# Modulated norm: factor on the scalar engine, scale and shift per feature behind the transposes

## The chip, the cores and the metric

The kernel runs on one core of a Trainium2 chip. The metric is the device time of one execution in microseconds (us); of several runs the median is given, and a profile belongs to one further execution. PE is TensorE (matrix multiplication), PEld its weight loads, DVE VectorE, ACT ScalarE, POOL GpSimd, SP SyncE. ACT, SP and POOL issue DMAs; in the profile q1 is the DMA queue of SP's issues, q10 that of ACT's, q0 that of POOL's. An engine name with a q (ACTq) is that engine's sequencer, which issues DMAs.

## The reference

Two blocks follow one another on 256 tokens of 1024 features, in fp32. The first has two layers of ffn, mixer, ffn, each with a residual and a layer norm. The second has two layers of a hybrid mixer and a feed-forward part (dense in layer 0, eight experts in layer 1); ahead of each stands a norm that is modulated by shift and scale rows, which are computed from a condition vector `c`:

```python
def rms_norm(x, g):
    x32 = x.astype(jnp.float32)
    y = x32 * lax.rsqrt(jnp.mean(jnp.square(x32), axis=-1, keepdims=True) + EPS)
    return (y * g.astype(jnp.float32)).astype(x.dtype)

def modulate(h, shift, scale):
    return h * (1.0 + scale) + shift

def second_block(x, c, ...):
    for layer in range(DEPTH):
        ...
        h = modulate(rms_norm(x, norm_mix_g[layer]), sh_m, sc_m)
        mix = hybrid_mixer(h, ...)
        x = x + gt_m * mix
        h = modulate(rms_norm(x, norm_ffn_g[layer]), sh_f, sc_f)
        ...
        x = x + gt_f * f
    return rms_norm(x, final_g)
```

The kernel folds `g * (1 + scale)` into one row beforehand, so that a modulated norm is x times r (one number per token) times a row, plus a row, where r is the inverse root of the mean square.

## The kernel before

The 256 tokens are two tiles, t = 0 and 1, of 128 rows by 1024 columns. To keep fp32 precision, every operand of a matmul is split in a high and a low part, and `mm3` (L175) makes three matmuls of them (L178, L179, L180). Weights come in on SP's queue in pieces of 1 MB; `weights` (L141) splits each with a Copy on ACT (L159) and a subtraction on DVE (L161). Activations are split by `split_to` (L182): a Copy on ACT (L184), a subtraction on DVE (L185).

Where a stage needs features on the partitions, `transpose_tile` (L203) turns one tile: twice four transposes on PE into one PSUM tile (L209), and each PSUM tile leaves in two parts of 128x256, each split by L184 and L185. `onward` (L1458) says what follows a stage's output: the new x is kept, the norm is applied, and `flip` transposes tile 0 at once, while tile 1's transposes are deferred to `X.complete()`, which the consumer (`toks` L279 or `ffn` L539) calls after its first matmuls on tile 0.

`ffn` (L496) makes hidden features in groups of 256 columns (f0 from 512 in the loop). Each group calls `feat_joint` (L245 and L246, into PSUM tiles of the name mm) for both weight halves, and the second weight multiplies an earlier group (`second`, into PSUM tiles of the name acc). At f0 = FF - 768 = 2048 it calls `finish.load()` (L558), which issues the loads that the residual needs; two groups and the tail follow. In the tail (L560, L562) tile 0's output is finished first, then tile 1's. `project` (L712) does the same for the mixers, with its call of load at L719.

`finish` is made by `residual_ln` (L568) or `gated_residual` (L903). The first loads ln_g and ln_b as broadcasts (`bcast` L289, an ACT-issued DMA of 512 KB at L291, kept in program order), adds the residual (L583), and applies the layer norm (L584 to L591). The second loads one gate row in the same way (`modrow` L486) and applies it (L916, L917). Both hand the tile to `then`.

`mod_norm` (L872) is used at three places, each with two tiles: behind the last ffn of the first block (residual_ln; the first mixer2 consumes it through `toks`), behind the first mixer2 (gated_residual; the dense ffn consumes it), and behind the dense ffn (gated_residual; the second mixer2 consumes it). At its first tile it issues two broadcasts of 512 KB, the shift and the scale row. Per tile, `rms` (L891) squares on ACT with a running sum (L897), DVE and POOL make r (L900, L298, L300), and then each half of 512 columns takes two passes on DVE:

```python
nc.vector.scalar_tensor_tensor(h[:, c], x[:, c], r, sc[:, c], op0=OP.mult, op1=OP.mult)   # L885
nc.vector.tensor_add(h[:, c], h[:, c], sh[:, c])                                          # L886
```

Two other places of this kernel hold patterns that the change also uses: `plan_columns` (L1109) transposes a 16x128 tile of mod rows into columns (L1113, L1115), its load being L1107 on POOL's queue; and the experts' gather applies a scale and a bias column with one Identity on ACT as data leaves PSUM (L1264), while L1168 is a Copy of a 128x1024 row tile with r as its scale.

Each engine runs its instructions in order. That order is set when the program is built: a scheduler hands out tile buffers from pools (PSUM: four of the name mm, four of the name acc; s4: 17 tiles of 4 KB per partition) and orders the instructions by what they depend on.

Of the kernel before, what the change touches and what calls it, by code (L numbers as in the profile page):

```python
# [17 lines left out]
F32 = mybir.dt.float32  # L18
# [4 lines left out]
AF = mybir.ActivationFunctionType  # L23
OP = mybir.AluOpType
# [53 lines left out]
class Kernel:  # L78
# [121 lines left out]
        x = X.parts[k // 2]  # L200
        return self.split_to(x[:, :, 0], x[:, :, 1], src)

    def transpose_tile(self, X, t, x):  # L203

        nc = self.nc
        for q in range(len(X.parts) // 2):
            p = self.mm([128, 4, 128])
            for j in range(4):
                nc.tensor.transpose(p[:, j, :], x[:, (4 * q + j) * 128:(4 * q + j + 1) * 128], self.ident)  # L209
            for i in range(2):  # L210
                part = X.parts[2 * q + i][:, :, :, t * 128:(t + 1) * 128]
                self.split_to(part[:, :, 0], part[:, :, 1], p[:, 2 * i:2 * i + 2, :])

    def transposed(self, x, nk=8):
        X = self.features(nk)
# [352 lines left out]
    def residual_ln(self, x, scale, i, then):  # L568


        nc = self.nc
        gb = []

        def load():
            gb.extend((self.bcast(self.a["ln_g"], i * D, D), self.bcast(self.a["ln_b"], i * D, D)))

        def finish(t, y):
            g, b = gb
            z = self.s4([128, D])
            st = self.s1(12)  # L580
            for n in range(2):
                c = slice(n * 512, (n + 1) * 512)
                nc.vector.scalar_tensor_tensor(z[:, c], y[n], scale / ALPHA, x[t][:, c], op0=OP.mult, op1=OP.add)  # L583
                nc.vector.bn_stats(st[:, n * 6:n * 6 + 6], z[:, c])  # L584
            mv = self.s1(2)
            nc.vector.bn_aggr(mv, st.rearrange("p (n s) -> p n s", s=6))
            r = self.rstd(mv[:, 1:2], LN_EPS / ALPHA ** 2)
            for n in range(2):
                c = slice(n * 512, (n + 1) * 512)
                nc.vector.scalar_tensor_tensor(z[:, c], z[:, c], mv[:, 0:1], g[:, c], op0=OP.subtract, op1=OP.mult)  # L590
                nc.vector.scalar_tensor_tensor(z[:, c], z[:, c], r, b[:, c], op0=OP.mult, op1=OP.add)  # L591
            then(t, z)

        finish.load = load
        return finish
# [275 lines left out]

    def mod_norm(self, l, i, then):  # L872

        nc = self.nc
        rows = []

        def norm(t, x):
            if not rows:
                rows.extend((self.modrow(l, i), self.modrow(l, i + 1)))
            sh, sc = rows  # L880
            h = self.s4([128, D])
            r = self.rms(x, h)
            for n in range(2):
                c = slice(n * 512, (n + 1) * 512)
                nc.vector.scalar_tensor_tensor(h[:, c], x[:, c], r, sc[:, c], op0=OP.mult, op1=OP.mult)  # L885
                nc.vector.tensor_add(h[:, c], h[:, c], sh[:, c])  # L886
            then(t, h)

        return norm

    def rms(self, x, scratch=None):  # L891
# [11 lines left out]
    def gated_residual(self, x, l, i, then):  # L903

        nc = self.nc
        rows = []

        def load():
            rows.append(self.modrow(l, i))

        def finish(t, y):
            g = rows[0]
            z = self.s4([128, D])
            for n in range(2):
                c = slice(n * 512, (n + 1) * 512)
                nc.vector.tensor_mul(z[:, c], y[n], g[:, c])  # L916
                nc.vector.tensor_add(z[:, c], z[:, c], x[t][:, c])  # L917
            then(t, z)

        finish.load = load  # L920
        return finish
# [536 lines left out]
    def onward(self, norm=None, fine=100):  # L1458


        x, X = [None, None], Features([])

        def flip(t, h):
            if not X.parts:
                X.parts = self.features(8).parts

            if t == 0:
                self.transpose_tile(X, t, h)
                self.fine = fine
            else:  # L1470
                X.later = lambda: self.transpose_tile(X, t, h)

        step = norm(flip) if norm else flip

        def then(t, z):
            x[t] = z
            step(t, z)

        return x, X, then

    def run(self, out):
# [68 lines left out]
```

## Time and profile before

| what | value |
|---|---|
| median of 3 runs | 2384.26 us (2381.79 to 2385.14) |
| the profiled execution | 2380.0 us |
| its span in the profile | 2378.2 us |
| mean granted PE clock | 0.996 |
| busy: PE, DVE, ACT, POOL | 98%, 81%, 63%, 3% of the span |
| DMA: SP's queue, ACT's queue | 71.0%, 1.8% of 16 engines' span |

The span is the time from the first to the last instruction in the profile; the execution's own time lies 1.8 us above it. Busy shares count an engine's instructions alone. A granted clock of 1.00 is full speed, 2.4 GHz; at about 0.5 it is at its lower level, 1.2 GHz. In the rows below, a timeline row gives the start, the busy time, engine, line, operation, what it writes and reads and the count, and in brackets the idle time before it with what ended that.

### The profile page before, as it was taken

The page shows a single profiled execution, that of the slowest core. Times are in us where ns is not written, and L with a number is a line of the kernel's source. Part 1 is how long each engine was busy: PE and PEld are TensorE (multiplying, and loading weights), DVE is VectorE, ACT ScalarE, POOL GpSimd, SP SyncE. Part 2 cuts the span into 40 slices and gives each one's busy share as a digit, 9 for nine tenths or more (in the row PEclk, how much of TensorE's full clock was granted, in tenths as well). Part 3 has the DMA queues.
Part 4 walks back from the last instruction along what each step waited for, and adds up shares of the span by engine and source line. Part 5 has one row for each costly group of instructions (what it writes and reads, how often), then busy time and mean ns, then how long its engine had stood idle before and what let it go on. Part 6 is the DMA issues. An engine that isn't in the chain of part 4 may idle for free.

```text
span 2378.2 us, 33917 instructions
## 1 busy us (share of the span) xinstructions
PE 2328.2 (98%) x12984; PEld 1992.0 (84%) x12984; DVE 1919.4 (81%) x2677; ACT 1494.7 (63%) x2172; POOL 64.5 (3%) x102
## 2 busy tenths in 40 slices
PE   8999999999999999999899999999999999999997
PEld 7888999888888999888788888878888887888876
DVE  6977877887787786887777667889989888898897
ACT  5555755564555664565475555778877777777674
POOL 0000000000000000000100001000000000000000
PEclk9999999999999999999999999999999999999999
DMA  8885446885787545677536565379999999999995
GB/s 287 301 315 178 142 161 203 273 288 182 261 286 245 183 163 184 232 258 258 181 103 227 178 203 184 116 274 329 358 336 333 351 345 342 359 334 353 365 347 208
DMA packets 318075, 607.92 MB, mean 256 GB/s; under 512 B 12976, under 2 KB 143550, under 8 KB 317904
## 3 DMA queue, kind: packets, MB, share of 16 engines
q1 hardware_dynamic: 310736, 590.52, 71.0%
q10 hardware_dynamic: 5696, 14.34, 1.8%
q8 instruction: 104, 1.70, 0.3%
q0 software_dynamic: 1472, 0.81, 0.1%
q14 instruction: 67, 0.55, 0.1%
HBM read 604.48 MB, written 1.15 MB: 255 GB/s over the span
## 4 chain that ended last, share of the span: by engine, by line
PE 39%; DVE 7%; ACT 3%; issue 2%; DMA 1%; POOL 0%; ACTq 0%; POOLq 0%; DVEq 0%
PE mm L179 7%; PE mm L180 7%; PE mm L178 7%; PE acc L179 4%; PE acc L180 4%; PE acc L178 4%; DVE wlo L161 3%; PE mm L245 3%; ACT whi L159 2%; PE mm L246 1%; PE mm L1290 1%; DVE s L185 0%; PE mm L1259 0%; DVE s L980 0%; PE mm L1339 0%
## 5 line engine op out<-in xcount | busy, mean ns | idle before, releaser
L161 DVE TENSOR_TENSOR wlo<-raw,whi 128x1024 fp32r<-128x1024 f32 (+1 forms) x1302 | 1231.6, 986 | 226.7 <-ACT whi L159 221.9
L159 ACT ACTIVATE whi<-raw 128x1024 fp32r<-128x1024 f32 (+1 forms) x1302 | 1063.4, 866 | 375.6 <-PE acc L180 95.4
L245 PE MATMUL mm<-s,whi 128*128 128x512 f32 x1440 | 510.1, 397 | 0.6 <-DVE cols L370 0.6
L179 PE MATMUL mm<-wlo,s 128*128 128x512 f32 (+1 forms) x1184 | 420.5, 356 | 3.0 <-DVE wlo L161 2.2
L178 PE MATMUL mm<-whi,s 128*128 128x512 f32 (+1 forms) x1184 | 418.8, 354 | 3.3 <-ACT s L184 2.9
L180 PE MATMUL mm<-whi,s 128*128 128x512 f32 (+1 forms) x1184 | 414.2, 351 | 1.4 <-DVE s L185 1.0
L246 PE MATMUL mm<-s,wlo 128*128 128x256 f32 x1440 | 404.1, 281 | 0.0
L179 PE MATMUL acc<-wlo,s 128*128 128x512 f32 x984 | 386.6, 395 | 1.5
L180 PE MATMUL acc<-whi,s 128*128 128x512 f32 x984 | 381.0, 392 | 0.6 <-DVE s L185 0.6
L178 PE MATMUL acc<-whi,s 128*128 128x512 f32 x984 | 377.0, 394 | 4.5 <-ACT s L184 4.5
L245 PEld LDWEIGHTS mm<-s,whi 128*128 128x128 f32 x1440 | 270.4, 188 | 67.8 <-issue 3.2
L246 PEld LDWEIGHTS mm<-s,wlo 128*128 128x128 f32 x1440 | 272.0, 189 | 2.3
L179 PEld LDWEIGHTS mm<-wlo,s 128*128 128x128 f32 x1184 | 225.3, 190 | 41.0 <-DVE wlo L161 13.8
L178 PEld LDWEIGHTS mm<-whi,s 128*128 128x128 f32 x1184 | 225.5, 190 | 35.6 <-ACT s L184 5.0
L180 PEld LDWEIGHTS mm<-whi,s 128*128 128x128 f32 x1184 | 225.0, 190 | 30.3 <-DVE s L185 1.8
L178 PE MATMUL mm<-s,whi 128*128 128x256 f32 x784 | 222.8, 285 | 1.5 <-ACT s L184 1.5
L178 PEld LDWEIGHTS acc<-whi,s 128*128 128x128 f32 x984 | 184.8, 188 | 47.0 <-ACT s L184 9.1
L179 PEld LDWEIGHTS acc<-wlo,s 128*128 128x128 f32 x984 | 185.1, 188 | 46.0 <-DVE wlo L161 9.8
L179 PE MATMUL mm<-s,whi 128*128 128x256 f32 x784 | 222.0, 283 | 0.0
L180 PE MATMUL mm<-s,wlo 128*128 128x256 f32 x784 | 221.9, 283 | 0.0
L180 PEld LDWEIGHTS acc<-whi,s 128*128 128x128 f32 x984 | 185.4, 188 | 40.8 <-DVE s L185 2.6
L178 PEld LDWEIGHTS mm<-s,whi 128*128 128x128 f32 x784 | 148.6, 190 | 3.2 <-ACT s L184 2.0
(317 smaller groups left out, 1990.6 us busy)
## 6 DMA issues: line engine op xcount, KB each, us to landing
raw<-in_moe_w_dram SPq DMA_DIRECT2D x261, 1024.0 KB, 6.2
raw<-in_ffn_w_dram SPq DMA_DIRECT2D x164, 1024.0 KB, 5.5
raw<-in_w_in_dram SPq DMA_DIRECT2D x60, 1024.0 KB, 5.0
raw<-in_ada_w_dram SPq DMA_DIRECT2D x48, 1024.0 KB, 5.3
raw<-in_w_out_dram SPq DMA_DIRECT2D x16, 1024.0 KB
s<-rows ACTq DMA_DIRECT2D x10, 512.0 KB, 7.6
raw<-in_w_branch_b_dram SPq DMA_DIRECT2D x4, 1024.0 KB
raw<-in_w_branch_a_dram SPq DMA_DIRECT2D x4, 1024.0 KB
```

The costliest lines, as they stand in the source:

```text
L159: nc.scalar.activation(h[:, c], x[:, c], AF.Copy)
L161: nc.vector.tensor_sub(l[:, c], x[:, c], h.bitcast(F32)[:, c])
L178: nc.tensor.matmul(out, lh, rh, start=start, stop=False, skip_group_check=skip)
L179: nc.tensor.matmul(out, lh, rl, start=False, stop=False, skip_group_check=skip)
L180: nc.tensor.matmul(out, ll, rh, start=False, stop=stop, skip_group_check=skip)
L245: nc.tensor.matmul(p, h, X.joint(k), start=k == 0, stop=False, skip_group_check=True)
L246: nc.tensor.matmul(p[:, 0, :], l, X(k)[0], start=False, stop=k == 7, skip_group_check=True)
L1290: nc.tensor.transpose(p[:, j, :], hid[:, j * 128:(j + 1) * 128], self.ident)
```

## The change

`mod_norm` no longer loads broadcast rows. It takes a tile `cols` of 128x16, and gets a `load` of its own, which the residual's `load` calls behind its own broadcasts: one DMA of 16 rows of 128 (shift and scale, 8 KB) on ACT's queue, a transpose on PE, a copy to `cols` on DVE. Per tile, ACT multiplies x by r (two Copies of 128x512) in place of the four DVE passes. `transpose_tile` gets `cols`, and where they are given, each 128x128 block leaves PSUM through an Identity on ACT with its scale and bias column into an SBUF tile y of the name s2; `split_to` then reads y in place of PSUM. The other users of `transpose_tile` are unchanged.

```diff
@@ -200,7 +200,7 @@
         x = X.parts[k // 2]
         return self.split_to(x[:, :, 0], x[:, :, 1], src)
 
-    def transpose_tile(self, X, t, x):
+    def transpose_tile(self, X, t, x, cols=None):
 
         nc = self.nc
         for q in range(len(X.parts) // 2):
@@ -209,7 +209,14 @@
                 nc.tensor.transpose(p[:, j, :], x[:, (4 * q + j) * 128:(4 * q + j + 1) * 128], self.ident)
             for i in range(2):
                 part = X.parts[2 * q + i][:, :, :, t * 128:(t + 1) * 128]
-                self.split_to(part[:, :, 0], part[:, :, 1], p[:, 2 * i:2 * i + 2, :])
+                y = p[:, 2 * i:2 * i + 2, :]
+                if cols is not None:
+                    y = self.s2([128, 2, 128])
+                    for j in range(2):
+                        k = 4 * q + 2 * i + j
+                        nc.scalar.activation(y[:, j, :], p[:, 2 * i + j, :], AF.Identity, scale=cols[:, 8 + k:9 + k],
+                                             bias=cols[:, k:k + 1])
+                self.split_to(part[:, :, 0], part[:, :, 1], y)
 
     def transposed(self, x, nk=8):
         X = self.features(nk)
@@ -573,6 +580,8 @@
 
         def load():
             gb.extend((self.bcast(self.a["ln_g"], i * D, D), self.bcast(self.a["ln_b"], i * D, D)))
+            if hasattr(then, "load"):
+                then.load()
 
         def finish(t, y):
             g, b = gb
@@ -871,21 +880,26 @@
 
     def mod_norm(self, l, i, then):
 
-        nc = self.nc
-        rows = []
+
+        nc = self.nc
+        cols = self.p1.tile([128, 16], F32, name="mod", bufs=2)
+
+        def load():
+            r = self.s1(128)[:16, :]
+            self.tc.keep_in_program_order(nc.scalar.dma_start(r, self.rows[l, 8 * i:8 * i + 16]))
+            p = self.mm([128, 16])
+            nc.tensor.transpose(p, r, self.ident[:16, :16])
+            nc.vector.tensor_copy(cols, p)
 
         def norm(t, x):
-            if not rows:
-                rows.extend((self.modrow(l, i), self.modrow(l, i + 1)))
-            sh, sc = rows
             h = self.s4([128, D])
             r = self.rms(x, h)
             for n in range(2):
                 c = slice(n * 512, (n + 1) * 512)
-                nc.vector.scalar_tensor_tensor(h[:, c], x[:, c], r, sc[:, c], op0=OP.mult, op1=OP.mult)
-                nc.vector.tensor_add(h[:, c], h[:, c], sh[:, c])
-            then(t, h)
-
+                nc.scalar.activation(h[:, c], x[:, c], AF.Copy, scale=r)
+            then(t, h, cols)
+
+        norm.load = load
         return norm
 
     def rms(self, x, scratch=None):
@@ -907,6 +921,8 @@
 
         def load():
             rows.append(self.modrow(l, i))
+            if hasattr(then, "load"):
+                then.load()
 
         def finish(t, y):
             g = rows[0]
@@ -1460,15 +1476,15 @@
 
         x, X = [None, None], Features([])
 
-        def flip(t, h):
+        def flip(t, h, cols=None):
             if not X.parts:
                 X.parts = self.features(8).parts
 
             if t == 0:
-                self.transpose_tile(X, t, h)
+                self.transpose_tile(X, t, h, cols)
                 self.fine = fine
             else:
-                X.later = lambda: self.transpose_tile(X, t, h)
+                X.later = lambda: self.transpose_tile(X, t, h, cols)
 
         step = norm(flip) if norm else flip
 
@@ -1476,6 +1492,8 @@
             x[t] = z
             step(t, z)
 
+        if norm:
+            then.load = step.load
         return x, X, then
 
     def run(self, out):
```

## Rows read from the trace of the kernel before

**Rows 1.** Busy time and share of each engine; the chain that ended last, by engine.

```profile
PE 2328.2 (98%) x12984; PEld 1992.0 (84%) x12984; DVE 1919.4 (81%) x2677; ACT 1494.7 (63%) x2172; POOL 64.5 (3%) x102
...
PE 39%; DVE 7%; ACT 3%; issue 2%; DMA 1%; POOL 0%; ACTq 0%; POOLq 0%; DVEq 0%
```

**Rows 2.** PE's waits: total us, times, longest us.

```profile
PE mm L209 <- DVE s L886: 10.1, 5, 5.6
```

**Rows 3.** Timeline of PE, first place, ahead of the transposes of tiles 0 and 1.

```profile
1153.36 1.23 PE L209 MATMUL mm<-ident,s 128*128 128x128 f32 x8 [1.57 <-DVE s L886]
...
1168.56 1.94 PE L209 MATMUL mm<-ident,s 128*128 128x128 f32 x8 [5.64 <-DVE s L886]
```

**Rows 4.** Windows: PE, PEld, DVE, ACT, POOL busy (count), PEclk, DMA share, GB/s.

```profile
1168.50:1172.70 4.20, 4.14 (x14) 3.67 (x15) 2.12 (x5) 1.43 (x4) 0.00 (x0) 0.51 0.03 10
1172.70:1177.00 4.30, 4.30 (x20) 3.50 (x20) 2.55 (x3) 3.18 (x3) 0.00 (x0) 1.00 0.14 26
```

**Rows 5.** Timeline of DVE, first place.

```profile
1151.20 1.41 DVE L885 SCALAR_TENSOR_TENSOR s<-s,t,s 128x512 f32<-128x512 f32 x2 [0.45 <-POOL t L300]
1152.53 1.29 DVE L886 TENSOR_TENSOR s<-s,s 128x512 f32<-128x512 f32 x2
...
1157.18 0.41 DVE L185 TENSOR_TENSOR s<-mm,s 128x256 fp32r<-128x256 f32 x1
1157.52 1.27 DVE L583 SCALAR_TENSOR_TENSOR s<-acc,s 128x512 f32<-128x512 f32 x2
```

**Rows 6.** Timelines of PE and DVE, second place.

```profile
1259.35 1.41 DVE L885 SCALAR_TENSOR_TENSOR s<-s,t,s 128x512 f32<-128x512 f32 x2 [2.22 <-DMA s<-rows]
...
1261.51 0.63 PE L209 MATMUL mm<-ident,s 128*128 128x128 f32 x4 [1.78 <-DVE s L886]
```

**Rows 7.** Groups of instructions by line and form: busy us, mean ns, idle before.

```profile
L159 ACT ACTIVATE whi<-raw 128x512 fp32r<-128x512 f32 x564 | 321.8, 623 | 206.7 <-PE acc L180 70.8 <-PE mm L179 43.9 <-PE mm L245 34.8
...
L184 ACT ACTIVATE s<-mm 128x256 fp32r<-128x256 f32 x116 | 41.6, 382 | 51.0 <-PE mm L209 33.7 <-DVE s L185 11.7 <-PE mm L1290 4.6
...
L184 ACT ACTIVATE s<-mm 128x512 fp32r<-128x512 f32 x40 | 23.8, 595 | 52.9 <-PE mm L1290 52.5
...
L1264 ACT ACTIVATE s<-mm,shsc 128x256 f32<-128x256 f32 x32 | 16.3, 562 | 13.4 <-PE mm L1259 13.4
...
L1168 ACT ACTIVATE s<-s,t 128x1024 fp32r<-128x1024 f32 x2 | 2.3, 1150 | 1.5 <-POOL t L300 1.5
```

**Rows 8.** Instructions of L1113: duration ns min/median/max, start.

```profile
L1113 PE MATMUL mm<-ident,t x1: 233/233/233, 1346.7 to 1346.7; 16*128 16x16 f32 x1
```

**Rows 9.** Timelines of ACT's issues and of PE, first and third place.

```profile
1110.36 0.45 ACTq L291 DMA_DIRECT2D s<-in_ln_b_dram  x1
...
1112.40 0.39 PE L245 MATMUL mm<-s,whi 128*128 128x512 f32 x1
1112.63 0.28 PE L246 MATMUL mm<-s,wlo 128*128 128x256 f32 x1
...
1411.94 0.33 ACTq L291 DMA_DIRECT2D s<-rows  x1
...
1414.37 0.39 PE L245 MATMUL mm<-s,whi 128*128 128x512 f32 x1
```

**Rows 10.** DMA queues in 1112:1113, 1113:1118, 1117:1118, 1258.3:1259.3, 1415:1418 (packets, MB, share).

```profile
q1 hardware_dynamic: 192, 0.39, 101.0%
...
q10 hardware_dynamic: 288, 1.05, 52.0%
...
q10 hardware_dynamic: 4, 0.01, 3.1%
...
q10 hardware_dynamic: 9, 0.02, 6.1%
...
q10 hardware_dynamic: 144, 0.52, 42.7%
...
q1 hardware_dynamic: 125, 0.22, 19.4%
```

## The prediction

> **What bounds the kernel now.** The page first [rows 1]: TensorE (PE) is busy for 98% of the span, and PE leads the chain that ended last, so the time falls only if one of PE's few pauses shrinks or PE gets less to do. The waits of PE come next, to see which pauses the change can reach [rows 2]: five waits, 10.1 us together, the longest 5.6 us, lie ahead of the transposes of L209 and end with L886, the second vector pass that the change removes. Then I read the timelines at the places where the modulated norm runs: site 1 (end of the last first-block ffn), site 2 (end of the first mixer2), site 3 (end of the dense ffn). At site 1 PE waits 1.57 us before tile 0's transposes and 5.64 us before tile 1's [rows 3]. After the long wait PE runs at a granted clock of 0.51, its lower level of 1.2 GHz, for 4.2 us, then at 1.00 [rows 4]: the same eight transposes take 1.94 us instead of 1.23 [rows 3], and half of 4.2 us, about 2 us, is lost. So site 1 holds some 9 us. At site 2 the wait is 1.78 us [rows 6]; the other two of the five, at site 3, share the rest, 10.1 - 1.57 - 5.64 - 1.78 = 1.1 us. All gains must come from these 10.1 us and the 2 us of clock.
>
> Why is the 5.64 us there? VectorE (DVE) starts tile 1's layer norm, L583, at 1157.52, directly behind the last split L185 of tile 0 [rows 5], though the accumulators of tile 1 had been finished by 1151.8, when PE fell idle [rows 3]. I read this as program order: the scheduler gives tile 1 its buffers after tile 0's. Keep this order in mind, since the new load comes into it too.
>
> **What is removed and added, on DVE and ACT.** Removed per tile: two L885 and two L886, 1.41 + 1.29 = 2.7 us by the two rows and about 2.6 us from start to end (1151.20 to 1153.82) [rows 5]. In their place ScalarE (ACT) does two row Copies of 128x512 with scale r. L1168, a Copy of 128x1024 with such a scale, takes 1.150 us [rows 7]; two halves I put at 1.35 us. The path to the transposes is shorter by 1.25 us. Six tiles free DVE of 15.6 us, but DVE counts only where PE waits for it.
>
> Added per tile: eight Identity of 128x128 with a scale and a bias column. The nearest row is L1264, 128x256 with two columns, 562 ns [rows 7]; L184 takes 382 ns for 128x256 against 595 ns for 128x512 in the same group of rows, so 128 columns less are worth about 0.107 us and the estimate is 0.455 us, 0.35 us from start to start. A part of an eviction was one L184; now it is two Identity and a Copy, about 1.15 us with its hand-over instead of 0.39. The first part comes 0.75 us later, which is on the path, since PE has just transposed. The next three are hidden where PE takes longer per part than 1.15 us: at sites 1 and 3 a part feeds six matmuls of 512 columns at 0.23 us (the distance from L245 to L246 [rows 9]), 1.38 us, so they are. At site 2 the matmuls have 256 columns; half of that, 0.7 us a part, covers nothing, and tile 1 there would lose 3 x 0.45 + 0.75 = 2.1 us if nothing else filled PE.
>
> The rows don't say that ACT is the slower engine for this: a Copy of 128x512 takes it 0.623 us, and a vector pass of that size takes DVE about 0.7 us [rows 5, 7]. The Trainium skill speaks against the change here: ScalarE: Activation LUTs, Rules for kernel authors, wants add and mul on VectorE and not on ScalarE, for VectorE's rate per element in bf16. By that rule ACT would become the limit, and the sum would be that of rival 3.
>
> **Gains, site by site.** Site 1, tile 0: the Copies start when r is there (1151.20 [rows 5]) and ACT's weight split under way is done (up to 0.6 us, half of which I take), so the path is about 1 us shorter; less 0.75 us, -0.3 us. Tile 1: -1.25 us for the passes, +0.75 us for the eviction, and half of DVE's 2.6 us arrives as an earlier L583: -1.8 us. The bounds are wide: -0.5 us if the slower splits hold L583 back, -7.5 us if all 5.64 us and the clock go; I am nearer to the first, since L583 follows tile 0's splits, which get slower. Site 2: -1.78 us at tile 0 (there DVE waited for the broadcast rows, 2.22 us [rows 6], which go), half of it kept after the slower eviction, and tile 1's loss about half covered: -0.5 us, bounds -1.8 to +2.1. Site 3: -0.3 us, bounds -1.1 to +0.75. Together -2.9 us.
>
> **The new load, the decisive part.** Per site two broadcasts of 512 KB go (the pairs of L291), and one DMA of 8 KB comes, r. It is moved: the broadcasts were issued with the norm, after the last group; r is issued with the residual's own rows, two feature groups and the tail earlier, behind them on ACT's queue. A transpose of r on PE (L1113 is such a one, 0.233 us [rows 8]) and a small DVE copy follow. Both are cheap: 3 x 0.23 = 0.7 us. Their wait is not. r's PSUM tile is taken ahead of those of the next feat_joint, and if buffers go out in order of first use, no later mm tile can pass it: PE, which runs in order, stands before the transpose until r is there, with all of feat_joint behind it; DVE's copy waits with L161's weight splits behind it.
>
> When is r there? At site 1 ln_g and ln_b are issued up to 1110.36 + 0.45; r would follow at about 1110.8. feat_joint begins at 1112.40 with no pause [rows 9]. In 1112 to 1113 only q1, SP's weights, moves (101%); the ACT queue's 288 packets (1.05 MB, ln_g and ln_b) come in 1113 to 1118, the last four after 1117 [rows 10]. r's packets stand behind these. At site 2 nine packets of the broadcast rows still ran after 1258.3 [rows 10], and the waiting L885 began at 1259.35 [rows 6]: I add 1.0 us from the last packet to the release. r is usable at 1118.1; PE could have gone on at 1112.6 after the transpose: stall 5.5 us. Bounds: 0.5 us if r overtakes, 6.5 us if the transpose stands before the group's end. After 5.6 us of idleness the clock cost 2 us [rows 3, 4]; I take 1.8 us more. Site 3: one gate row ahead of r, issued at 1411.94, moved in 1415 to 1418: its 42.7% and q1's 19.4% of the engines' time [rows 10], done without a gap, end at about 1416.9; feat_joint begins at 1414.37 [rows 9]: (1416.9 + 1.0) - 1414.6 = 3.3 us, and 0.5 us for the clock (between site 2, where 1.78 us cost nothing, and site 1); bounds 0 to 5.5. Site 2: a gate row too, but there the load falls into the last projection, whose accumulations need no new mm tile and run on beside it: 0.8 us, bounds 0 to 3.
>
> Sum: 5.5 + 1.8 + 3.3 + 0.5 + 0.8 + 0.7 = +12.6 us, less 2.9 = **+9.7 us**. On the profiled execution's 2380.0 us (span 2378.2 and 1.8 around it) that is 2389.7; that execution lies 4.3 us under the median of 2384.26, so the forecast is 2394.0 us. A difference under 0.2%, 4.8 us, can't be told from none.
>
> **Rivals.**
> 1. The load is hidden: r, being 8 KB, lands early or its transpose is placed later. For it: r is 8 KB behind 512 KB pieces, and the page tells nothing of such a load on ACT's queue; against: q10's rows. Then 0.7 - 2.9 = -2.2 us: 2382, no measurable change.
> 2. Faster: r hidden, and L583 of tile 1 moves by all 2.6 us. Site 1: -0.3 - (2.6 + 1.25 - 0.75) - 2.0 of clock = -5.4; sites 2 and 3 -1.8; transposes +0.7: -6.5 us, 2377.8. It decides if r is usable by about 1112.6 and L583 starts before 1156. For it: DVE is busy without a gap at site 1; against: the order of buffers.
> 3. ACT is the path, without the stall: row Copies queue behind L159 and gain nothing, each of six first parts costs 0.75 us, site 2 loses 0.45 x 3 twice: 4.5 + 2.7 + 0.7 = +7.9 us, 2392.2.
>
> **Chances.** Forecast 0.62; rival 1 0.18; rival 2 0.12; rival 3 0.08. From them: faster 0.12, same 0.20, slower 0.68. The stall alone spans 2388 to 2400 (all upper bounds with hardly any gain); the range takes in rival 1 and leaves out rival 2: 2380 to 2400.
>
> **What would show it.** Right: in the waits of PE a new wait of the r transpose on the DMA, 5 to 6 us at site 1 and about 3 us at site 3, just before feat_joint of the last but one group, with a lower granted clock after it at site 1; PE's waits for L886 gone and replaced by shorter ones for ACT's row Copies (about 4 us left before tile 1 of site 1); Identity near 0.45 us; ACT's busy time up by some 31 us (6 x (8 x 0.455 + 1.35) and a little), DVE's down by 15.6. Wrong: r lands within 2 us of its issue, feat_joint runs ahead of the r transpose, or tile 1's L583 starts 2 us sooner.

## The result, and the profile after

The changed kernel takes 2396.38 us (median of 5 runs, 2393.72 to 2398.45) against 2384.73 us of the kernel before (5 runs on the same chip). The ratio is 1.0056, 95% interval 1.0045 to 1.0066, so 0.56% or some 13.3 us slower (10.7 to 15.7); the two medians lie 11.65 us apart. The forecast was 2394.0 us in 2380 to 2400: slower, by the load's stall. The profiled execution took 2397.67 us, its span 2395.9 us.

The page of the changed kernel, parts 1 and 3: busy time of the engines, then packets, MB and share of ACT's DMA queue.

```profile
PE 2341.2 (98%) x12987; PEld 2001.3 (84%) x12987; DVE 1905.6 (80%) x2656; ACT 1516.8 (63%) x2232; POOL 67.7 (3%) x102
...
q10 hardware_dynamic: 4928, 11.22, 1.4%
```

Against [rows 1] DVE has 13.8 us less, ACT 22.1 us more, ACT's queue moves 3 MB less. All three are what the change is said to do, and none of them says why the time grew. PE's instructions grew by three, its busy time by 13 us: part of PE's work ran at a lower clock.

The waits of PE in the changed kernel, longest in total first (us in total, times, longest us):

```profile
PE mm L891 <- DMA t<-rows: 8.0, 2, 4.7
PE mm L178 <- ACT s L184: 7.5, 6, 3.3
PE mm L209 <- ACT s L899: 5.9, 5, 2.5
```

The waits of L209 for L886 [rows 2], 10.1 us, have become 5.9 us for ACT's row Copies (L899), and a new first line stands above them: the transpose of r (L891) waits for r's DMA, in two waits of 8.0 us together. The second line was 4.5 us in three waits before. The timeline of PE at the two places:

```profile
1117.41 0.39 PE L180 MATMUL acc<-whi,s 128*128 128x512 f32 x1
1122.47 0.25 PE L891 MATMUL mm<-ident,t 16*128 16x16 f32 x1 [4.67 <-DMA t<-rows]
1122.65 0.80 PE L252 MATMUL mm<-s,whi 128*128 128x512 f32 x1
...
1432.00 0.20 PE L891 MATMUL mm<-ident,t 16*128 16x16 f32 x1 [3.30 <-DMA t<-rows]
```

L252 is L245 of before: the transpose stands exactly between the accumulation and the feat_joint that followed it without a pause [rows 9], and nothing passes it. The windows of PE around these waits (PEclk is the third number from the end):

```profile
1117.60:1122.40 4.80, 0.20 (x1) 0.00 (x0) 1.90 (x3) 1.80 (x4) 0.00 (x0) 1.00 0.82 326
1122.40:1126.50 4.10, 4.03 (x14) 3.47 (x15) 0.77 (x2) 0.00 (x0) 0.00 (x0) 0.58 0.43 113
...
1432.00:1437.00 5.00, 5.00 (x20) 4.29 (x21) 0.77 (x2) 0.20 (x1) 0.00 (x0) 0.66 0.56 179
```

PE is idle, and in the 4 to 5 us behind each wait its granted clock is 0.58 and 0.66: part of both stretches runs at the lower level.

Two executions differ in more than the change, so the 17.7 us between the two spans were laid out by landmarks, the same instruction's start in both timelines:

| landmark | before | after | lag | step |
|---|---|---|---|---|
| ln_g issued, site 1 | 1109.99 | 1115.23 | 5.2 | 5.2 |
| in feat_joint behind the r transpose | 1114.04 | 1125.81 | 11.8 | +6.5 |
| accumulation behind tile 1's transposes, site 1 | 1176.90, 1177.13 | 1189.56, 1190.69 | 12.7, 13.6 | +1.3 |
| last projection of the first mixer2 | 1248.33 | 1262.73 | 14.4 | +1.3 |
| end of site 2 | 1276.54 | 1290.66 | 14.1 | -0.3 |
| in feat_joint behind the r transpose, site 3 | 1417.06 | 1436.48 | 19.4 | +5.3 |
| behind site 3 | 1471.74 | 1491.54 | 19.8 | +0.4 |
| end of the span | 2378.2 | 2395.9 | 17.7 | -2.1 |

The first 5.2 us lie where every engine has the same instructions in the same order in both kernels. About 1.5 us of them arise near 17 us, where PE's 256-column matmuls still started 0.21 us apart in the changed kernel's execution and already 0.12 us apart in the other (the granted clock is recorded as 1.00 in both), and 3 us near 273 us, where the granted clock was 0.75 in 270 to 275 us and 0.57 in the next 5 us, against 1.00 and 1.00 before, with PE busy throughout in both. The +1.3 us before the last projection and the -2.1 us at the end lie in stretches without an instruction of the change too. Behind tile 1's transposes at site 1 the two kernels order their matmuls differently, so that step is taken from the middle of two landmarks. What is left at the change's own places is 6.5 + 1.3 - 0.3 + 5.3 + 0.4 = 13.2 us, and 11.8 of it are the two loads.

Why r is late is seen on ACT's timeline at site 1 (start, duration of the issue) and in the DMA of two windows, 1118.7 to 1121.2 and 1121.2 to 1122:

```profile
1115.23 0.33 ACTq L298 DMA_DIRECT2D s<-in_ln_g_dram  x1
1115.60 0.45 ACTq L298 DMA_DIRECT2D s<-in_ln_b_dram  x1
1116.15 0.53 ACTq L889 DMA_DIRECT2D t<-rows  x1
```

```profile
DMA packets 309, 1.06 MB, mean 424 GB/s; under 512 B 32, under 2 KB 32, under 8 KB 309
...
q10 hardware_dynamic: 257, 0.99, 96.3%
...
DMA packets 63, 0.07 MB, mean 87 GB/s; under 512 B 32, under 2 KB 48, under 8 KB 63
...
q10 hardware_dynamic: 63, 0.07, 24.4%
```

The row "under 512 B" counts the small packets that close a transfer. Between 512 B and 2 KB there is no packet in the first window and 48 - 32 = 16 in the second: these are r's 16 rows of 512 B. They start after 1 MB of ln_g and ln_b has gone, and that moved only as SP's weights ran out: in 1118 to 1119 SP's queue took 87.8% of the engines' time and ACT's 16.9%, in 1119 to 1120 2.3% and 102.4%. r is 8 KB and had been issued at 1116.15; it moved at 1121.2 to 1121.8, and PE went on at 1122.47, 0.7 us after its last packet. The Trainium skill, DMA: Bandwidth & Descriptors, Two DMAs through the same engine are not ordered, says that descriptors of one queue of one DMA engine start in order; the 16 packets behind the 1 MB agree.

The norm itself, site 1, timeline of PE:

```profile
1165.73 1.36 PE L209 MATMUL mm<-ident,s 128*128 128x128 f32 x8 [2.52 <-ACT s L899]
1167.94 0.80 PE L178 MATMUL mm<-whi,s 128*128 128x512 f32 x1 [0.84 <-ACT s L184]
...
1181.04 1.27 PE L209 MATMUL mm<-ident,s 128*128 128x128 f32 x8 [1.98 <-ACT s L899]
1183.25 0.50 PE L178 MATMUL mm<-whi,s 128*128 128x512 f32 x1 [0.94 <-ACT s L184]
```

Against [rows 3] tile 1's wait fell from 5.64 to 1.98 us, but tile 0's rose from 1.57 to 2.52 us, and behind each set of transposes there is now a wait of 0.8 to 0.9 us for the first part's three ACT instructions. From tile 0's transposes to tile 1's it is 15.3 us, 15.2 before: what tile 1 waited less, PE spent on tile 0's matmuls at the lower clock (granted 0.53 in 1168 to 1174). The timeline of DVE shows where tile 1's layer norm stands:

```profile
1169.93 0.42 DVE L185 TENSOR_TENSOR s<-s,s 128x256 fp32r<-128x256 f32 x1 [0.58 <-ACT s L184]
1170.27 0.68 DVE L592 SCALAR_TENSOR_TENSOR s<-acc,s 128x512 f32<-128x512 f32 x1
1171.53 0.42 DVE L185 TENSOR_TENSOR s<-s,s 128x256 fp32r<-128x256 f32 x1 [0.57 <-ACT s L184]
```

Tile 1's layer norm (L592, L583 of before) still starts behind tile 0's splits, now the third instead of the fourth [rows 5], 4.5 us after tile 0's transposes instead of 4.2: between the splits DVE now waits 0.57 to 0.58 us each for ACT.

### The profile page after: what moved, and what is told of

The parts are those of the page before. It is cut to its first block, busy times and chain, and to the rows that moved or that the text cites. A ratio compares the mean times of both kernels' runs of the same rounds, so it can differ in the third digit from the quotient of the medians.

```text
span 2395.9 us, 33946 instructions
## 1 busy us (share of the span) xinstructions
PE 2341.2 (98%) x12987; PEld 2001.3 (84%) x12987; DVE 1905.6 (80%) x2656; ACT 1516.8 (63%) x2232; POOL 67.7 (3%) x102
## 3 DMA queue, kind: packets, MB, share of 16 engines
HBM read 601.36 MB, written 1.15 MB: 251 GB/s over the span
## 4 chain that ended last, share of the span: by engine, by line
PE 40%; DVE 5%; ACT 3%; issue 2%; DMA 1%; POOL 0%; ACTq 0%; POOLq 0%; DVEq 0%
PE mm L179 7%; PE mm L178 7%; PE mm L180 7%; PE acc L179 4%; PE acc L180 4%; PE acc L178 4%; PE mm L252 3%; DVE wlo L161 3%; ACT whi L159 2%; PE mm L253 1%; PE mm L1306 1%; PE mm L1275 1%; POOL t L307 0%; DVE s L996 0%; PE mm L1355 0%
## 5 line engine op out<-in xcount | busy, mean ns | idle before, releaser
L252 PE MATMUL mm<-s,whi 128*128 128x512 f32 x1440 | 513.0, 399 | 0.6 <-DVE cols L377 0.6
L252 PEld LDWEIGHTS mm<-s,whi 128*128 128x128 f32 x1440 | 271.7, 189 | 68.2 <-issue 2.1
```

The lines of the kernel that those rows point to most:

```text
L252: nc.tensor.matmul(p, h, X.joint(k), start=k == 0, stop=False, skip_group_check=True)
```

## The experiments

Each was timed in 5 rounds beside the kernel before; ratios are to that. "Late transpose" below is the second.

**1. r fetched a stage earlier** (sites 1 and 2; site 3 as in the change).

```diff
+        def fetch():
+            r16.append(self.s1(128)[:16, :])
+            self.tc.keep_in_program_order(nc.scalar.dma_start(r16[0], self.rows[l, 8 * i:8 * i + 16]))
+
+        if l == 0:
+            fetch()
+
         def load():
-            r = self.s1(128)[:16, :]
-            self.tc.keep_in_program_order(nc.scalar.dma_start(r, self.rows[l, 8 * i:8 * i + 16]))
+            if not r16:
+                fetch()
             p = self.mm([128, 16])
...
```

> For the first two places r's DMA is issued a whole stage earlier, when mod_norm is made; the transpose of r and the copy stay where the change has them, and the third place keeps the change's load. Theory (PE stands before the transpose of r until r's DMA has landed behind the broadcasts): the wait of 4.67 us at the first place and the half clock behind it go, 6.5 us, while the third place keeps its wait of about 3.3 us; so about 2390 us against 2396.4 for the change. Rival (the load is cheap; the eviction through ACT costs the time): no change, 2395 to 2398.

Measured: 2388.76 us, ratio 1.0023 (1.0014 to 1.0031). PE's timeline, site 1 and site 3:

```profile
1114.91 0.23 PE L900 MATMUL mm<-ident,t 16*128 16x16 f32 x1
...
1421.95 0.20 PE L900 MATMUL mm<-ident,t 16*128 16x16 f32 x1 [3.50 <-DMA t<-rows]
```

The transpose at site 1 has no wait, the one at site 3 keeps it. The theory gave 2390, the rival 2395 to 2398: the stall is the load's.

**2. Late transpose.**

```diff
         def load():
-            p = self.mm([128, 16])
-            nc.tensor.transpose(p, r, self.ident[:16, :16])
-            nc.vector.tensor_copy(cols, p)
...
         def norm(t, x):
+            if t == 0:
+                p = self.mm([128, 16])
+                nc.tensor.transpose(p, r16[0], self.ident[:16, :16])
+                nc.vector.tensor_copy(cols, p)
```

> r's DMA is issued where the change issues it, but its transpose and the copy to cols stand at the first tile's norm, after all feature groups. Theory: no PSUM tile of the feature groups is behind r's any more, both waits (4.67 and 3.30 us) and the half clock after them go, 11.8 us: about 2384.6 us, the same as the kernel before within 0.2%. Rival (eviction through ACT): 2393 to 2397. A second rival (the norm itself gains, as I had put it at 2.9 us): 2381 to 2382.

Measured: 2382.41 us, ratio 0.9995 (0.9986 to 1.0004), the same as before; the rival with the eviction is out, while the theory and the second rival lie too close together to be told apart by this. The DMA is issued where the change issues it; PE just doesn't meet it early. So the position of the transpose on PE is the price, and not the load. It also gives the worth of everything else in the change: -1.2 us, between -3.3 and +1.0. PE's timeline before tile 1, site 1:

```profile
1169.91 1.70 PE L209 MATMUL mm<-ident,s 128*128 128x128 f32 x8 [4.62 <-ACT s L902]
1172.12 0.79 PE L178 MATMUL mm<-whi,s 128*128 128x512 f32 x1 [0.51 <-ACT s L184]
```

Where tile 0 isn't delayed, tile 1's wait is nearly the 5.64 us of before [rows 3].

**3. The load alone**, in the kernel before: `load` as in the change, `cols` unused, rows and vector passes kept.

> The kernel before with the change's load added and its result unused: the two vector passes, the broadcast rows and the plain eviction stay. Theory: the load alone costs 11.8 us, so about 2396.5 us, with PE waits for the transpose of r of 4 to 5 us and about 3.3 us. Rival (the eviction through ACT is what costs): 2385 us, with no or short waits at the transpose of r.

Measured: 2394.2 us, ratio 1.0040 (1.0026 to 1.0054), with PE's waits as in the change:

```profile
PE mm L209 <- DVE s L905: 10.8, 5, 5.6
PE mm L891 <- DMA t<-rows: 8.0, 2, 4.6
```

The load without the change costs 9.5 us (0.40%; 6.2 to 12.9), the whole change 13.3 us (10.7 to 15.7); the theory had 11.8. The intervals overlap, so what the rest of the change costs can't be read from this pair. The rival that the eviction costs it is out: here the eviction is that of before, and the loss is there all the same.

**4. r ahead of the broadcasts.**

```diff
         def load():
-            gb.extend((self.bcast(self.a["ln_g"], i * D, D), self.bcast(self.a["ln_b"], i * D, D)))
             if hasattr(then, "load"):
                 then.load()
+            gb.extend((self.bcast(self.a["ln_g"], i * D, D), self.bcast(self.a["ln_b"], i * D, D)))
```

and the same in the gated residual.

> The change with r's DMA issued ahead of the residual's broadcasts in place of behind them. Theory in its exact form (r stands behind the broadcasts in ACT's queue, and they behind SP's weights): r then only waits for SP's weights, whose packets left off about 2.4 us before the broadcasts did; the wait at the first place falls from 4.67 to about 2.3 us, at the third from 3.3 to about 2 us, and the half clock may go; 2388 to 2393 us. Rival (the wait is a fixed latency or SP's weights alone, the order in the queue does nothing): waits as before the edit, 4.7 and 3.3 us, and 2396 us.

Measured: 2387.76 us, ratio 1.0017 (1.0008 to 1.0026). The time lies just under what the theory gave (2388 to 2393), and the waits don't fit it: they are gone, not halved. ACT's and PE's timelines:

```profile
1109.37 0.34 ACTq L889 DMA_DIRECT2D t<-rows  x1
```

```profile
1117.88 0.23 PE L891 MATMUL mm<-ident,t 16*128 16x16 f32 x1
```

r left 6 us before the broadcasts, which were issued at 1115.40, as late as in the change. Ahead of them r is not held back, so in the change it was the order kept on ACT's queue that held its issue back as well (that the broadcasts themselves wait for their buffers is my reading; no row shows it). So this run doesn't part "behind the broadcasts' packets" from "issued behind them"; the packets shown above do the first. It is 0.22% slower than the late transpose. Of the 6.2 us between the two profiled executions 3 us lie ahead of site 1's norm and 1.6 us at it, where POOL's power is slow as in the change (below); that the power makes them is not shown, and the rest isn't settled.

**5. DVE made to wait for r.**

```diff
-            r = self.rms(x, h)
+            r = self.s1(1)
+            nc.vector.tensor_copy(r, self.rms(x, h))
```

> The change, with r (the norm's factor) copied once by DVE before ACT uses it, so that DVE has an instruction waiting for POOL's power instead of running on. In the change that power took 3.19 us at the first tile of the first place, while DVE ran four weight splits without a gap, and in the kernel before 0.86 us. Theory (POOL's power is held up by DVE's unbroken run): the power falls to about 0.9 us there, PE's wait before the tile's transposes from 2.52 to about 0.5 us and the half clock behind it goes; 2 to 4 us less than the change, 2392 to 2394 us; the waits for r's load (4.7 and 3.3 us) stay. Rival (the 3.19 us have another cause): the power stays near 3.2 us and the time at 2395 to 2398 us.

The reason for this run is a row of POOL in the changed kernel, the power that makes r for tile 0 at site 1, and ACT's Copies behind it; before, the same power took 0.86 us:

```profile
1161.73 3.19 POOL L307 TENSOR_TENSOR t<-t,mhalf 128x1 f32<-128x1 f32 x1 [3.70 <-DVE t L305]
```

```profile
1164.95 1.33 ACT L899 ACTIVATE s<-s,t 128x512 f32<-128x512 f32 x2 [2.36 <-POOL t L307]
```

Measured: 2399.3 us, ratio 1.0063 (1.0049 to 1.0078), no faster than the change. POOL's and PE's timelines:

```profile
1163.59 0.86 POOL L307 TENSOR_TENSOR t<-t,mhalf 128x1 f32<-128x1 f32 x1 [3.70 <-DVE t L305]
```

```profile
1165.50 1.27 PE L209 MATMUL mm<-ident,s 128*128 128x128 f32 x8 [0.43 <-ACT s L900]
...
1181.06 1.33 PE L209 MATMUL mm<-ident,s 128*128 128x128 f32 x5 [4.91 <-ACT s L900]
```

The instruction came out as forecast, the time did not: what tile 0 no longer waits, tile 1 waits, as in run 2. Between the two profiles site 1 is only 0.6 us shorter than in the change. A delay of tile 0 costs little as long as tile 1's chain starts late anyway.

**6. The eviction on two engines** (on the late transpose): ACT's Identity writes the high part from PSUM, DVE computes the same from PSUM and subtracts.

```diff
-                        nc.scalar.activation(y[:, j, :], p[:, 2 * i + j, :], AF.Identity, scale=cols[:, 8 + k:9 + k],
-                                             bias=cols[:, k:k + 1])
-                self.split_to(part[:, :, 0], part[:, :, 1], y)
...
+                    nc.scalar.activation(h[:, j, :], p[:, 2 * i + j, :], AF.Identity, scale=cols[:, 8 + k:9 + k],
+                                         bias=cols[:, k:k + 1])
+                    nc.vector.tensor_scalar(y[:, j, :], p[:, 2 * i + j, :], cols[:, 8 + k:9 + k], cols[:, k:k + 1],
+                                            op0=OP.mult, op1=OP.add)
+                nc.vector.tensor_sub(l, y, h.bitcast(F32))
```

> The late transpose of the run before last, and the eviction shared: ACT's Identity writes the high part straight out of PSUM, DVE computes the same values out of PSUM beside it and subtracts. Theory (after each tile's transposes PE waits 0.5 to 0.94 us for the three ACT instructions of the first part): that wait falls by about 0.7 us per tile, three tiles or more of the six being exposed, so 2 to 4 us less than the late transpose alone, 2378.5 to 2380.5 us, faster than the kernel before by 0.1 to 0.2%. Rival (the ends of these waits are set elsewhere, by tile 1's layer norm): 2382 us as without.

Measured: 2385.74 us, ratio 1.0011 (1.0000 to 1.0022): by 0.16% slower than the late transpose, the intervals just overlapping; in any case no gain, a miss. DVE's timeline at site 1, then PE's at sites 1 (two rows) and 3:

```profile
1157.80 1.23 DVE L161 TENSOR_TENSOR wlo<-raw,whi 128x1024 fp32r<-128x1024 f32 x1 [0.34 <-ACT whi L159]
1158.94 0.40 DVE L221 TENSOR_SCALAR s<-mm,mod 128x128 f32<-128x128 f32 x1
1159.38 0.42 DVE L223 TENSOR_TENSOR s<-s,s 128x256 fp32r<-128x256 f32 x1
```

```profile
1159.86 0.50 PE L180 MATMUL mm<-whi,s 128*128 128x512 f32 x1 [1.79 <-DVE s L223]
...
1171.91 1.33 PE L209 MATMUL mm<-ident,s 128*128 128x128 f32 x5 [2.88 <-ACT s L906]
...
1472.46 1.27 PE L209 MATMUL mm<-ident,s 128*128 128x128 f32 x8 [2.05 <-ACT s L906]
```

DVE's share of the eviction stands between weight splits of up to 1.23 us, and the low part comes 1.8 us late, where the wait for ACT had been 0.94 us. Yet site 1 is no place of the loss: tile 1's wait there is 2.88 us instead of 4.62, and laid out by landmarks the site is 1 us shorter than in run 2's profile. The 4.7 us lost lie at site 2 (3.1 us, with a new wait of 1.11 us for DVE's low part) and site 3 (1.6 us), where tile 1's transposes now wait 2.05 us.

**7. The factor on DVE** (on the late transpose).

```diff
-                nc.scalar.activation(h[:, c], x[:, c], AF.Copy, scale=r)
+                nc.vector.tensor_scalar(h[:, c], x[:, c], r, None, op0=OP.mult)
```

> The late transpose, with the factor r applied by DVE in one pass per half instead of ACT's Copy. Theory (on the path to the transposes one pass costs about the same on either engine, 0.7 us a half; what counts is one pass in place of two): within 2 us of the late transpose alone, 2380.5 to 2384.5 us. Rival (ACT's Copy is what shortens the path): 1.25 us per exposed tile more, 2385 to 2388 us.

Measured: 2383.39 us, ratio 1.0001 (0.9989 to 1.0013), no difference from the late transpose. It doesn't matter here whose the one pass is. What one pass in place of two is worth isn't shown by it, since tile 1's wait at site 1 stays (4.78 us). In this profile r's late transpose also waited 1.15 us for its DMA at site 2, which no other run with the late transpose shows.

**8. Tile 1's layer norm ahead** (on the late transpose). `flip` for tile 0 (its features and transpose_tile) is kept back as `then.flush` and called from `finish` of tile 1, behind its residual and statistics:

```diff
                 nc.vector.bn_stats(st[:, n * 6:n * 6 + 6], z[:, c])
+            if t == 1 and hasattr(then, "flush"):
+                then.flush()
```

and in the gated residual behind its two passes.

> The late transpose of r, and in program order tile 1's residual and its statistics (first half of the layer norm; at the gated residuals the two passes on the rows) stand ahead of tile 0's transposes instead of behind them, at the three places of the modulated norm. Theory (tile 1's layer norm starts behind tile 0's splits only by program order, and that makes PE's wait of 4.6 us before tile 1's transposes at the first place and the half clock behind it): the wait falls below 2 us, the norm of tile 1 begins before tile 0's splits; 3 to 6 us less than the late transpose alone, 2376.5 to 2379.5 us, faster than the kernel before by 0.1 to 0.25%. Rival (something else sets it, as the engines' speed): the wait stays above 4 us and the time at 2382 us.

Measured: 2378.29 us, ratio 0.9985 (0.9975 to 0.9996). PE's timeline at sites 1 and 2:

```profile
1165.43 1.27 PE L209 MATMUL mm<-ident,s 128*128 128x128 f32 x8
1167.64 0.50 PE L178 MATMUL mm<-whi,s 128*128 128x512 f32 x1 [0.94 <-ACT s L184]
...
1263.21 0.58 PE L178 MATMUL mm<-whi,s 128*128 128x256 f32 x1 [2.37 <-ACT s L184]
```

The wait before tile 1 at site 1 is gone, and the half clock with it: that wait was program order. At site 2 the turn costs a new wait. Laid out against run 2's profile, the turn gains 6.9 us at site 1 and gives back 2.4 and 1.5 us at sites 2 and 3.

**9. The same turn in the kernel before.**

> The kernel before, with the same turn of the program order and nothing else. Theory (DVE is without a gap at the first place there, since it makes the two vector passes too, so an earlier start of tile 1's layer norm delays tile 0's passes): the wait before tile 1's transposes falls from 5.6 to 2 to 3.5 us, that before tile 0's grows by up to 2 us; 1 to 3 us less than the kernel before, 2379.5 to 2381.5 us, which may not be told from it. Rival (DVE is no limit there): as much as in the run beside it, 3 to 6 us less.

Measured: 2379.83 us, ratio 0.9993 (0.9984 to 1.0002), within the theory. At site 1 the wait before tile 1 is 3.02 us, tile 0's stays at 1.57 us, and PE has a new one of 1.16 us for a split of tile 0. With the turn at all three places the change's idea (run 8) and the kernel before (run 9) lie 1.5 us apart by the medians, which can't be told from none.

**10 and 11. The turn at site 1 alone**, on the late transpose and in the kernel before: the gated residual calls flush at once.

> The late transpose, with tile 1's residual and statistics ahead of tile 0's transposes at the first place alone. Theory (the turn gains about 6.9 us at the first place and gives back 2 us each at the second and third, where PE then waits 2.4 and 1.6 us for the first split of tile 0 behind the gated residual): 2 to 4 us less than with the turn at all three, 2374.5 to 2376.5 us, faster than the kernel before by 0.25 to 0.35%. Rival (what the others give back is made up elsewhere): 2378 us.

> The kernel before, with the turn at the first place alone. Theory (DVE, which makes the two vector passes as well, gives part of the gain back in the splits of tile 0): 1 to 4 us less than before, 2378 to 2381 us, and slower than the run beside it by 2 to 5 us, which would be what the change's row factor on ACT is worth once the turn is made. Rival (the turn alone is the gain, and the ACT factor is worth nothing): the same time as the run beside it.

Measured: 2374.15 us, ratio 0.9954 (0.9940 to 0.9969), and 2381.25 us, ratio 0.9987 (0.9977 to 0.9998). The first is faster than both kernels: by the ratios 11 us less than before, 24 us less than the change as it was made. It gained a little more than its theory gave (0.46% for 0.25 to 0.35%), and the 7.1 us between the two runs are more than the 2 to 5 expected. The windows of run 10 around tile 0's and tile 1's transposes, and DVE's timeline, then PE's of run 11:

```profile
1159.00:1163.00 4.00, 2.97 (x15) 2.26 (x16) 4.00 (x9) 4.00 (x13) 0.00 (x0) 1.00 0.78 261
1163.00:1169.00 6.00, 6.00 (x28) 4.95 (x27) 5.38 (x12) 3.84 (x9) 3.65 (x5) 1.00 0.68 208
1169.00:1176.00 7.00, 5.96 (x29) 4.34 (x28) 1.91 (x4) 6.77 (x16) 2.29 (x5) 1.00 0.45 162
```

```profile
1157.79 0.68 DVE L592 SCALAR_TENSOR_TENSOR s<-acc,s 128x512 f32<-128x512 f32 x1
1159.59 0.67 DVE L592 SCALAR_TENSOR_TENSOR s<-acc,s 128x512 f32<-128x512 f32 x1
1161.38 0.41 DVE L185 TENSOR_TENSOR s<-s,s 128x256 fp32r<-128x256 f32 x1
```

```profile
1156.49 0.50 PE L180 MATMUL mm<-whi,s 128*128 128x512 f32 x1 [1.16 <-DVE s L185]
...
1167.32 1.23 PE L209 MATMUL mm<-ident,s 128*128 128x128 f32 x8 [3.02 <-DVE s L888]
```

L592 now stands ahead of L185, PE keeps its full clock through the site, and no wait there is over 1 us. With DVE's two passes (run 11) 3.02 us stay. So once nothing else holds tile 1 back at site 1, the change's idea is worth 7.1 us by the medians of these two runs, on one chip; about 5 us of that are seen at site 1 between the two profiles, and where the rest lies isn't shown. Without the turn and without the stall (run 2) it can't be told from nothing.

## Why the prediction was right, point by point

- **The load's stall.** Right in mechanism, place and order of size. Site 1: 5.5 us forecast (5 to 6 as the sign of being right), 4.67 us measured; site 3: 3.3 us, measured 3.30 us. My 1.0 us from the last packet to the release was 0.7 us. Runs 1, 2 and 3 remove it, move it and make it alone.
- **Its clock.** 1.8 us forecast at site 1, 1.6 us measured (the step of 6.5 less 4.67 and the transpose's 0.25). At site 3 I took 0.5 us, and 5.3 - 3.3 - 0.2 = 1.8 us were lost: a mis-sized term. The wait of 3.3 us cost the clock as much as the one of 4.7 us.
- **Site 2's load**, 0.8 us forecast: no wait for r's DMA there in the change. The accumulations covered it wholly.
- **The norm's gains**, -2.1, -0.5 and -0.3 us: here steps failed. At site 1 it was +1.3 us. The step "half of DVE's 2.6 us arrives as an earlier L583" failed: L592 came 4.5 us after tile 0's transposes instead of 4.2, since the slower splits ate what the passes freed. Run 8 shows what stood in the way: with the program order turned, L592 no longer follows the splits and the wait is gone. "About 4 us left before tile 1" came out as 1.98 us only because tile 0 was late; in run 2, where it isn't, it is 4.62 us. Tile 0's "-0.3 us" failed in the change, where POOL's power took 3.19 us; with 0.86 us in run 5 the wait was 0.43 us, as I had reckoned. Sites 2 and 3 were within 0.7 us of the forecast. Without the stall the whole was -1.2 us (run 2) where I had -2.9 + 0.7.
- **Prices.** Identity 0.455 us estimated, 0.462 us measured; row Copies 1.35 us for two, measured 1.33 us. Instructions of L217 in the changed kernel, duration ns min/median/max:

```profile
L217 ACT ACTIVATE s<-mm,mod x48: 439/462/490, 1166.4 to 1487.3; 128x128 f32<-128x128 f32 x48
```

- ACT's busy time rose by 22 us, not 31: I added durations, and instructions in a row overlap on the engine (three of L217 in a row took 1.16 us, not 3 x 0.46). DVE's fell by 13.8 us, not 15.6.
- **Rival 1** (load hidden) is the time of run 2, **rival 2** (tile 1's layer norm free) became real only when the program order was turned, at 0.9954. **Rival 3** (ACT as the path of the whole loss) is out: run 2 keeps all of ACT's work and loses nothing, run 7 takes the factor off ACT and gains nothing, run 6 takes part of the eviction off it, gains 1 us at site 1 and loses more at the others. The Trainium skill, ScalarE: Activation LUTs, Rules for kernel authors, prefers VectorE for add and mul; neither run that moved such work to DVE was faster than run 2.
- **The order of buffers.** I had read from L583's place behind the last split that order sets it. Run 8 turned the order and the wait went, so that reading is shown now; in the forecast it was an inference from one row.

Forecast +9.7 us, measured 13.3 us (10.7 to 15.7), 11.65 by the medians. By the landmarks of the two profiles the difference is the norm at site 1 (3.4 us) and site 3's clock (1.3 us) above all, less a shorter loss at site 1's load (1 us) and none at site 2's. That the time lies in 2380 to 2400 says little, since rival 1 lay in it too; the waits' places and sizes, and runs 1 to 3, are what bear the forecast out.

## What to carry to other kernels

A small load can be as late as what its queue holds ahead of it, and the first instruction that needs it can stop everything behind it on its engine: issue it early if you like, but put its consumer where its result is used, not where it is loaded. Before a pass is made cheaper, ask which order releases the next tile; here taking 2.6 us of vector work per tile off DVE gained nothing measurable until tile 1's layer norm stood ahead of tile 0's splits at the first place, and some 5 to 7 us after that. And lay two profiles out by landmarks before explaining their difference: 5 of 17.7 us here came before the first changed instruction.

## What the runs showed of the hardware

- POOL's power on 128x1 took 0.55 to 0.56 us with DVE idle beside it, and 3.19 and 3.20 us in the change and in run 4, at the same place, ending 0.4 us after a run of four weight splits on DVE, beside which it ran. In run 5, where DVE waits for it, it took 0.86 us. The Trainium skill, SBUF — State Buffer, SBUF: two separate sides, says that VectorE and GpSimd have a pair of ports in common, which the one that starts first holds for its whole instruction, a VectorE instruction with two SBUF inputs among them where the GpSimd one reads SBUF; a weight split has two. The 3.19 us and run 5 agree. Run 2 doesn't show it as plainly: there DVE ran five splits in a row at that place, and the power took 0.86 us, ending 0.41 us after the first of them. So an unbroken run of splits alone doesn't make it slow, and what decides which engine gets in between two splits stays open.
- PE's clock fell in one execution and not in another around the same wait: 2.15 us of idleness in the first mixer2 left the clock at 1.00 in the kernel before, while in the changed kernel it was 0.71 in the 5 us with that wait. Windows of the kernel before, then of the changed one (PEclk is the third number from the end):

```profile
1235.00:1240.00 5.00, 2.85 (x18) 2.43 (x18) 2.77 (x5) 4.00 (x6) 0.00 (x0) 1.00 0.04 11
```

```profile
1250.00:1255.00 5.00, 2.85 (x8) 2.27 (x8) 4.18 (x6) 2.59 (x5) 0.00 (x0) 0.71 0.06 13
```

- Near 273 us it fell in the changed kernel's execution without any wait, as told above. So two single spans of this kernel can lie some us apart by the clock, before any change is met: 5.2 us did here.
